# The projection up by seven block products instead of eight, on activations normed beforehand

## The chip, the core and the metric

The kernel runs on one core of one Trainium2 chip. The core has a matrix engine (TensorE, PE in the profile), a vector engine (VectorE, DVE), an engine for functions of one operand (ScalarE, ACT), a general engine (GpSimd, POOL) and a queue that starts transfers (SyncE, SP). The working memory is SBUF with 128 partitions; matrix products land in PSUM, which has eight banks of 512 fp32 columns here. The metric is the device time of one execution in microseconds; runs are compared by their median.

## The reference

A residual block of a streaming encoder on a sequence of 512 tokens behind 16 meta tokens, with model width 1024: a mixer, then a gated feed-forward network with a causal convolution of width 3, with RMS norms before each and at the end. The change concerns the feed-forward half. Cut to it:

```python
def rms_norm(x, gain):
    xf = x.astype(jnp.float32)
    y = xf * lax.rsqrt(jnp.mean(xf * xf, axis=-1, keepdims=True) + RMS_EPS)
    return (y * gain.astype(jnp.float32)).astype(x.dtype)

def conv_ffn(h, w_up, conv_w, conv_b, w_down):
    u = causal_dwconv(h @ w_up.astype(h.dtype), conv_w, conv_b)
    gate, up = u[..., :D_FF], u[..., D_FF:]          # D_FF = 2816
    return (jax.nn.silu(gate) * up) @ w_down.astype(h.dtype)
...
        h = h + hybrid_mixer(rms_norm(h, norm_mix_w[layer]), ...)
        h = h + conv_ffn(rms_norm(h, norm_ffn_w[layer]), ffn_w_up[layer], ffn_conv_w[layer],
                         ffn_conv_b[layer], ffn_w_down[layer])
    return rms_norm(h, norm_final_w)[:, N_META:]
```

All is fp32, and the products are made exact enough by splitting both factors.

## The kernel before

Activations lie transposed: 128 channels on the partitions, the tokens as columns. The width of 1024 is `KT` = 8 row blocks, the inner width of 2816 is `FT` = 22. Only the last `TO` = 514 of the 528 columns are still needed after the mixer (512 tokens and two for the convolution); they are worked on in two halves `HO` of 258 and 256 columns, each of which fits a PSUM bank.

Each factor of a product is split into a rounded part `hi` and a remainder `lo`. ACT writes `hi`, DVE writes `lo = raw - hi`: for weights in `weights` (L120 to L133, the lines 131 and 132), for activations in `split` (L1067). `product` (L135) then runs three matmuls per row block: hi by hi (L139), hi by lo (L140), lo by hi (L141). The pools `whi` and `wlo` (L98, L99) have two buffers each, `wraw` has three; a weight tile is 128 output channels by 1024, 512 KB, loaded by SP.

The stages that the change touches follow one another:

- Branch products (L1090 to L1146): GDN's, then fox's weights against the two branches. `ofT` holds fox's output; `mg` gathers both branches and is split to `mh`, `ml`. The first three fox tiles are begun ahead (L1124 to L1130), while the last pair of heads is still being worked on.
- Projection out (L1155 to L1169): eight tiles, each in both halves. The eviction (L1160) adds the product to the residual `h2`, which was loaded before (L1107). Then the channel gain is multiplied in (L1162), the result is split to `uh`, `ul`, and squares are summed on POOL (L1169). The factor `rstd2` of the norm (`norm_scale`, L152) is finished later, beside the first products of the next stage.
- Projection up (L1191 to L1210): for each of 22 channel blocks a gate tile and an up tile. Each takes one weight tile and 2 x 24 matmuls on `uh`, `ul`, which hold the activations without the norm's factor; the eviction on DVE multiplies it in (L1197). The convolution is one ACT and two DVE steps (L1200 to L1202), then `Silu` for the gate, the product of both on DVE (L1209), and the split to `fh`, `fl` at once.
- Projection down (L1237 to L1263): eight tiles of 22 row blocks, matmuls of 512 columns, weights in three chunks `c`; the eviction adds to `h2`, the final norm follows.

The order of each engine's instructions is made by a scheduler from priorities; without one, program order counts. Tiles in a pool wait for the release of what lay in their memory before (`reuse_waits="tile"`).

Of the kernel before, what the change touches and what calls it, by code (L numbers as in the profile page):

```python
# [12 lines left out]
F32 = mybir.dt.float32  # L13
F32R = mybir.dt.float32r
# [72 lines left out]
def hybrid_block(ctx: ExitStack, tc: tile.TileContext, xT, w_in, w_bg, w_bf, w_out, w_up, w_down,  # L87
# [10 lines left out]
    whi = ctx.enter_context(tc.tile_pool(name="whi", bufs=2))  # L98
    wlo = ctx.enter_context(tc.tile_pool(name="wlo", bufs=2))  # L99
# [35 lines left out]
    def product(ps, wh, wl, xh, xl, k0, k, a, b, first=True, last=True, w0=0):  # L135

        for i in range(k):
            ws = slice((w0 + i) * P, (w0 + i + 1) * P)
            pe.matmul(ps, wh[:, ws], xh[:, k0 + i, a:b], start=first and i == 0, stop=False)  # L139
            pe.matmul(ps, wh[:, ws], xl[:, k0 + i, a:b], start=False, stop=False)  # L140
            pe.matmul(ps, wl[:, ws], xh[:, k0 + i, a:b], start=False, stop=last and i == k - 1)  # L141
# [10 lines left out]
    def norm_scale(pl, y, parts, n):  # L152

        v = pl.tile([P, n], F32, tag="nv", bufs=1, name="nv")
        t = pl.tile([P, n], F32, tag="nt", bufs=1, name="nt")
# [6 lines left out]
        dve.scalar_tensor_tensor(y, t, 1.5, y, op0=ALU.add, op1=ALU.mult)  # L162
# [8 lines left out]
    qd = dram.tile([12, P, T], F32, name="qd")  # L171

# [779 lines left out]
    ofp = ctx.enter_context(tc.tile_pool(name="ofp", bufs=1, reuse_waits="tile"))  # L952
# [149 lines left out]
    late = ctx.enter_context(tc.tile_pool(name="late", bufs=1, reuse_waits="tile"))  # L1102
    uh = late.tile([P, KT, TO], F32R, name="uh")
    ul = late.tile([P, KT, TO], F32R, name="ul")
    h2 = late.tile([P, KT, TO], F32, name="h2")
    rstd2 = late.tile([P, TO], F32, name="rstd2")
    for k in range(KT):  # L1107
        nc.sync.dma_start(h2[:, k, :], xT[:, k, OFF:])
    with ExitStack() as bctx:
        bp = bctx.enter_context(tc.tile_pool(name="bp", bufs=1, reuse_waits="tile"))  # L1110
        rf = rb_ctx.enter_context(tc.tile_pool(name="rf", bufs=1, side="right", reuse_waits="tile"))
        ofl, ofh = (rf.tile([P, 4, TO], F32R, name=n) for n in ("ofl", "ofh"))
        mh, ml = (bp.tile([P, KT, TO], F32R, name=n) for n in ("mh", "ml"))
        for p in range(4):
            if p < 3:
                split(ofh[:, p], ofl[:, p], ofT[:, p])
            else:
                with tc.high_priority(offset=FOXP):
                    split(ofh[:, p, 0:258], ofl[:, p, 0:258], ofT[:, p, 0:258])
                    with behind(dve):  # L1120
                        last_divide(256, SEQ)
                    split(ofh[:, p, 258:], ofl[:, p, 258:], ofT[:, p, 258:])
# [25 lines left out]
        lps = ctx.enter_context(tc.tile_pool(name="lps", bufs=5, space=PSUM, reuse_waits="tile"))  # L1148
# [3 lines left out]

        acc = bp.tile([P, TO], F32, name="acc2")
        ln_exp_table()
        for e in range(KT):  # L1155
            wh, wl = weights(w_out[e].rearrange("p k c -> p (k c)"), KT, f"o{e}")
            for a, b in HO:
                ps = lbank("ps_o")
                product(ps[:, :b - a], wh, wl, mh, ml, 0, KT, a, b)
                dve.scalar_tensor_tensor(h2[:, e, a:b], ps[:, :b - a], 0.5, h2[:, e, a:b], op0=ALU.mult, op1=ALU.add)  # L1160
            ug = btmp("ug")
            act.activation(ug, h2[:, e], AF.Copy, scale=prm[:, PG_FFN + e:PG_FFN + e + 1])  # L1162
            split(uh[:, e], ul[:, e], ug)
            if e == 0:
                act.activation(acc, h2[:, e], AF.Square)
            else:
                sq = btmp("sq2")
                act.activation(sq, h2[:, e], AF.Square)
                pool.tensor_tensor(acc, acc, sq, op=ALU.add)  # L1169
        parts = []  # L1170
        for a, b in HO:
            ps = mmp.tile([P, 512], F32, tag="mm", name="ps_n2")[:, :b - a]
            pe.matmul(ps, ones, acc[:, a:b], start=True, stop=True)
            parts.append((ps, a, b))
        with tc.high_priority():
            norm_scale(bp, rstd2, parts, TO)
        note("h2", h2.rearrange("p a b -> p (a b)"))
    rb_ctx.close()
    mix_ctx.close()


    with ExitStack() as uctx:
        ap = uctx.enter_context(tc.tile_pool(name="ap", bufs=1, reuse_waits="tile"))
        u2 = uctx.enter_context(tc.tile_pool(name="u2", bufs=9, reuse_waits="tile"))
        fh = ap.tile([P, FT, SEQ], F32R, name="fh")
        fl = ap.tile([P, FT, SEQ], F32R, name="fl")

        def utmp(name):
            return u2.tile([P, TO], F32, tag="tmp", name=name)

        def up_tile(i):  # L1191
            wh, wl = weights(w_up[i].rearrange("p k c -> p (k c)"), KT, f"up{i}")
            y = utmp(f"u{i}")
            for a, b in HO:
                ps = lbank("ps_up")
                product(ps[:, :b - a], wh, wl, uh, ul, 0, KT, a, b)
                dve.tensor_tensor(y[:, a:b], ps[:, :b - a], rstd2[:, a:b], op=ALU.mult)  # L1197
            w = prm[:, PG_FC + 3 * i:PG_FC + 3 * i + 3]
            o = utmp(f"v{i}")[:, 0:SEQ]
            act.activation(o, y[:, 2:], AF.Identity, scale=w[:, 2:3], bias=prm[:, PG_FB + i:PG_FB + i + 1])  # L1200
            dve.scalar_tensor_tensor(o, y[:, 1:TO - 1], w[:, 1:2], o, op0=ALU.mult, op1=ALU.add)
            dve.scalar_tensor_tensor(o, y[:, 0:SEQ], w[:, 0:1], o, op0=ALU.mult, op1=ALU.add)  # L1202
            return o

        for f in range(FT):
            g = up_tile(2 * f)
            act.activation(g, g, AF.Silu)
            u = up_tile(2 * f + 1)
            dve.tensor_tensor(g, g, u, op=ALU.mult)  # L1209
            split(fh[:, f], fl[:, f], g)  # L1210
            if f == 0:
                note("act0", g)
# [9 lines left out]
        def residual(e, ps, a, b):  # L1222

            h3 = h2[:, e, 2 + a:2 + b]
# [3 lines left out]
            else:  # L1228
                sq = utmp("sq3")[:, 0:b - a]
# [7 lines left out]
        for e in range(KT - 1):  # L1237
# [126 lines left out]
```

## Time and profile before

| | us |
|---|---|
| median of 3 runs | 876.53 |
| lowest and highest | 873.74, 877.31 |
| the profiled execution | 877.7 |
| its span, first to last instruction | 875.8 |

The profile is of one execution. Its page gives busy times of the engines and cuts the span into forty equal slices of 21.9 us; each digit is the busy share in tenths. Other views group the instructions of a stretch by line and shape with the mean duration and the idle time ahead of them, list them in order of time, or add them up by stretch. A row of the timeline reads: start, duration, engine, line, operation, what is written from what, shapes, count, and in brackets how long the engine had been idle and what released it. Matmuls are pipelined, so that their recorded durations overlap; the distance of their starts is their cost. Of 7088 matmuls 2112 belong to the projection up.

### The profile page before, as it was taken

How to read it: one execution, taken by the hardware profiler on the slowest of the kernel's cores; microseconds unless marked ns; L12 is line 12 of the kernel's file. 1: busy time of each engine (PE TensorE's matmuls, PEld its weight loads, DVE VectorE, ACT ScalarE, POOL GpSimd, SP SyncE). 2: the span in 40 equal slices, each digit the busy share in tenths (PEclk: the TensorE clock that was granted, in tenths of full speed). 3: DMA queues.
4: the chain of work that ended last, by engine and by line, in shares of the span. 5: the costliest groups of instructions: out<-in, count | busy, mean ns of one | idle time of the engine just before them, and what ended most of it. 6: DMA issues, size and time to landing. Idle time of an engine off the chain costs nothing. (4 is left out here: it accounts for less than half of the span.)

```text
span 875.8 us, 17084 instructions
## 1 busy us (share of the span) xinstructions
PE 839.6 (96%) x7088; PEld 801.0 (91%) x7088; DVE 585.5 (67%) x1066; ACT 392.6 (45%) x611; POOL 140.5 (16%) x167
## 2 busy tenths in 40 slices
PE   7978999999999999899999999999999999999995
PEld 7977999999999999788999999999999999888884
DVE  7999998697266678787654676677766677232324
ACT  6655554523433485855354454434444344332321
POOL 4353575100000201100522100000000000010113
PEclk9999999999999999989999999999999999999997
DMA  7312233627432341335623223333223332333322
GB/s 229 107 49 73 74 97 99 149 93 176 127 116 74 92 140 61 98 103 150 218 98 97 89 83 95 97 97 95 80 92 98 97 96 77 99 91 107 91 67 96
DMA packets 52240, 91.27 MB, mean 104 GB/s; under 512 B 24438, under 2 KB 27646, under 8 KB 52164
## 3 DMA queue, kind: packets, MB, share of 16 engines
q1 hardware_dynamic: 51060, 89.14, 33.9%
q8 instruction: 55, 0.90, 0.5%
q10 hardware_dynamic: 1104, 1.05, 0.4%
q14 instruction: 21, 0.17, 0.1%
HBM read 80.01 MB, written 10.16 MB: 103 GB/s over the span
## 5 line engine op out<-in xcount | busy, mean ns | idle before, releaser
L140 PE MATMUL ps_in<-xl,hi_in 128*128 128x264 f32 (+2 forms) x720 | 197.8, 285 | 2.5 <-DVE xl L264 2.5
L139 PE MATMUL ps_in<-xh,hi_in 128*128 128x264 f32 (+2 forms) x720 | 197.4, 287 | 1.7 <-ACT hi_in L131 1.2
L140 PE MATMUL ps_up<-ul,hi_up 128*128 128x256 f32 (+1 forms) x704 | 198.7, 282 | 0.0
L141 PE MATMUL ps_in<-xh,lo_in 128*128 128x264 f32 (+2 forms) x720 | 196.7, 286 | 1.9 <-DVE lo_in L132 1.9
L141 PE MATMUL ps_up<-uh,lo_up 128*128 128x256 f32 (+1 forms) x704 | 198.4, 282 | 0.0
L139 PE MATMUL ps_up<-uh,hi_up 128*128 128x256 f32 (+1 forms) x704 | 198.0, 282 | 0.0
L140 PEld LDWEIGHTS ps_in<-xl,hi_in 128*128 128x128 f32 x720 | 132.8, 188 | 4.0 <-DVE xl L264 3.1
L139 PEld LDWEIGHTS ps_in<-xh,hi_in 128*128 128x128 f32 x720 | 132.0, 188 | 4.5 <-ACT hi_in L131 1.9
L141 PEld LDWEIGHTS ps_in<-xh,lo_in 128*128 128x128 f32 x720 | 132.0, 188 | 3.8 <-DVE lo_in L132 2.6
L139 PEld LDWEIGHTS ps_up<-uh,hi_up 128*128 128x128 f32 x704 | 133.0, 189 | 0.0
L141 PEld LDWEIGHTS ps_up<-uh,lo_up 128*128 128x128 f32 x704 | 132.8, 189 | 0.0
L140 PEld LDWEIGHTS ps_up<-ul,hi_up 128*128 128x128 f32 x704 | 132.7, 188 | 0.0
L1197 DVE TENSOR_TENSOR u<-ps_up,rstd 128x258 f32<-128x258 f32 x88 | 37.2, 425 | 56.6 <-PE ps_up L141 56.6
L139 PE MATMUL ps_dn<-fh,hi_dn 128*128 128x512 f32 (+1 forms) x198 | 73.5, 371 | 0.0
L140 PE MATMUL ps_dn<-fl,hi_dn 128*128 128x512 f32 (+1 forms) x198 | 73.0, 369 | 0.0
L141 PE MATMUL ps_dn<-fh,lo_dn 128*128 128x512 f32 (+1 forms) x198 | 73.0, 369 | 0.0
L132 DVE TENSOR_TENSOR lo_dn<-raw_dn,hi_dn 128x1024 fp32r<-128x1024 f32 (+1 forms) x25 | 29.0, 1160 | 61.2 <-ACT hi_dn L131 61.2
L131 ACT ACTIVATE hi_in<-raw_in 128x1024 fp32r<-128x1024 f32 x43 | 45.0, 1054 | 51.3 <-PE ps_in L140 33.4
L1232 POOL TENSOR_TENSOR acc<-acc,sq 128x512 f32<-128x512 f32 (+1 forms) x7 | 11.2, 1607 | 353.1 <-ACT sq L1230 353.1
L131 ACT ACTIVATE hi_up<-raw_up 128x1024 fp32r<-128x1024 f32 x44 | 46.7, 1061 | 37.8 <-PE ps_up L140 28.3
L132 DVE TENSOR_TENSOR lo_up<-raw_up,hi_up 128x1024 fp32r<-128x1024 f32 x44 | 53.9, 1225 | 14.3 <-ACT hi_up L131 14.3
L131 ACT ACTIVATE hi_dn<-raw_dn 128x1024 fp32r<-128x1024 f32 (+1 forms) x25 | 24.8, 993 | 74.9 <-PE ps_dn L140 70.0
(339 smaller groups left out, 1655.8 us busy)
## 6 DMA issues: line engine op xcount, KB each, us to landing
raw_up<-w_up SPq DMA_DIRECT2D x44, 512.0 KB, 3.5
raw_in<-w_in SPq DMA_DIRECT2D x43, 512.0 KB, 4.0
raw_dn<-w_down SPq DMA_DIRECT2D x17, 512.0 KB, 3.5
gd<-g SPq DMA_DIRECT2D x16, 257.0 KB, 4.2
gt<-gd SPq DMA_DIRECT2D x16, 257.0 KB, 2.7
raw_o<-w_out SPq DMA_DIRECT2D x8, 512.0 KB, 3.5
raw_dn<-w_down SPq DMA_DIRECT2D x8, 384.0 KB, 3.1
xr<-xT SPq DMA_DIRECT2D x8, 264.0 KB, 4.4
```

Of the source, the lines that this page charges most:

```text
L131: act.activation(hi[:, a:a + step], raw[:, a:a + step], AF.Copy)
L132: (eng or dve).tensor_tensor(lo[:, a:a + step], raw[:, a:a + step], hi[:, a:a + step].bitcast(F32), op=ALU.subtract)
L139: pe.matmul(ps, wh[:, ws], xh[:, k0 + i, a:b], start=first and i == 0, stop=False)
L140: pe.matmul(ps, wh[:, ws], xl[:, k0 + i, a:b], start=False, stop=False)
L141: pe.matmul(ps, wl[:, ws], xh[:, k0 + i, a:b], start=False, stop=last and i == k - 1)
L1197: dve.tensor_tensor(y[:, a:b], ps[:, :b - a], rstd2[:, a:b], op=ALU.mult)
L1232: pool.tensor_tensor(acc[:, a:b], acc[:, a:b], sq, op=ALU.add)
```

## The change

The 22 pairs of a gate tile and an up tile are taken as a matrix of two by two blocks: gate and up are the two block rows, the first and the last four of the eight row blocks of the width are the two block columns. The activations are two by two blocks too: the same halves of the width, by two halves of the columns, of 258 each, which overlap by two columns (0 to 258, 256 to 514). Strassen's algorithm in Winograd's form computes the four output blocks by seven block products of 4 x 3 matmuls instead of eight.

- Weights: POOL makes four sums of 512 columns per pair (`load_pair`). The operands of the seven products are a11 and a12 (chunk X, the gate tile as loaded), the third sum and a22 (Y), s2 and s1 (Z) and the fourth sum (W); each chunk is split by ACT and DVE (`split_chunk`), up to two chunks ahead.
- Activations: since sums of blocks go into the products, the norm's factor and the gain are multiplied in beforehand (`unit`), blocks are combined on DVE (`combine`), and each of the seven is split (`operand`). They stay in `MH`, `ML` for the stage.
- To have them early, the projection out leaves the second halves of its last three tiles to the end, and the norm of the first half runs meanwhile. The products 1 and 2, which need the first half alone, are run for three pairs ahead (`AHEAD`).
- PSUM: products 1, 6 and 7 are accumulated in one bank, 5 and 3 in another; in between ACT and DVE read the sums that the outputs need. PE's order is written out (`seq`, `manual_schedule`).
- The gating product goes from DVE to POOL (`F_POOL`), into `f` in fp32; its split to `fh`, `fl` is made behind the stage, since the operands fill the memory.
- `h2` is loaded later, written to DRAM (`hd`) behind the projection out and read back for the projection down. There the first two tiles run chunk by chunk in turn. The last down tile no longer loads its first chunk twice. `whi` and `wlo` are made anew with three buffers behind `ofT`'s release.

```diff
+    w_ctx.close()
+    whi = ctx.enter_context(tc.tile_pool(name="whi", bufs=3, reuse_waits="tile"))
+    wlo = ctx.enter_context(tc.tile_pool(name="wlo", bufs=3, reuse_waits="tile"))
...
+        def unit(name, k0, a, gain):
+            u = tp.tile([P, 4, HB], F32, tag="t", bufs=6, name=name)
+            for k in range(4):
+                dve.scalar_tensor_tensor(u[:, k], h2[:, k0 + k, a:a + HB], gain[:, k0 + k:k0 + k + 1], rstd2[:, a:a + HB],
+                                         op0=ALU.mult, op1=ALU.mult)
+            return u
+
+        def operand(j, u, sign=1.0):
+            for k in (slice(0, 2), slice(2, 4)):
+                act.activation(MH[j][:, k], u[:, k], AF.Copy, scale=sign)
+                if sign == 1.0:
+                    dve.tensor_tensor(ML[j][:, k], u[:, k], MH[j][:, k].bitcast(F32), op=ALU.subtract)
...
         for e in range(KT):
+            w = weights(w_out[e].rearrange("p k c -> p (k c)"), KT, f"o{e}")
+            sq = out_tile(e, *w, *HO[0])
+            if e < KT - 3:
+                out_tile(e, *w, *HO[1])
             else:
+                last[e] = w
+        ffn_norm(sq, *HO[0])
+        for e, w in last.items():
+            sq = out_tile(e, *w, *HO[1])
+            nc.sync.dma_start(hd[e], h2[:, e, 2:])
...
+        with tc.high_priority(offset=SOON_W):
+            n11 = unit("n11", 0, 0, ngain)
+            operand(1, n11)
+            b21 = unit("b21", 4, 0, gain)
+            operand(2, b21)
+        ffn_norm(sq, *HO[1])
...
+    seq = [(j, i) for i in range(AHEAD) for j in (1, 2)]
+    for i in range(FT + 1):
+        for j, d in ((1, 0), (2, 0), (7, 1), (4, 1), (6, 0), (5, 0), (3, 1)):
+            if 0 <= i - d < FT and not (j < 3 and i < AHEAD):
+                seq.append((j, i - d))
...
+    def load_pair(i):
...
+        for o, x, y in ((s1, a21, a22), (s2, s1, a11), (q3, a11, a21), (Q[i], s2, a12)):
+            pool.tensor_tensor(o, x, y, op=ALU.add)
...
+    def seven(ps, j, i, start=True):
+        wh, wl = splits[chunk_of[j], i]
+        for k in range(4):
+            ws = slice((place[j] + k) * P, (place[j] + k + 1) * P)
+            for w, x in ((wh, MH), (wh, ML), (wl, MH)):
+                pe.matmul(ps, w[:, ws], x[j][:, k], start=start and k == 0 and w is wh and x is MH,
+                          stop=k == 3 and w is wl, skip_group_check=not start)
...
+            g = conv(YG.pop(i), 2 * i)
             act.activation(g, g, AF.Silu)
+            u = conv(YU.pop(i), 2 * i + 1)
+            (pool if F_POOL else dve).tensor_tensor(f[:, i], g, u, op=ALU.mult)
...
+    b12, b22 = unit("b12", 0, HB - 2, gain), unit("b22", 4, HB - 2, gain)
...
+    t1 = combine("t1", b12, n11, ALU.add)
+    t2 = combine("t2", b22, t1, ALU.subtract)
+    operand(6, t2)
+    operand(5, t1)
+    operand(7, combine("m7", b12, b22, ALU.subtract))
+    operand(4, combine("m4", b21, t2, ALU.subtract))
+    operand(3, b22, -1.0)
...
+        for k in range(FT):
+            fh.append(ap.tile([P, SEQ], F32R, name=f"fh{k}"))
+            fl.append(ap.tile([P, SEQ], F32R, name=f"fl{k}"))
+            split(fh[k], fl[k], f[:, k])
+        h3t = ap.tile([P, KT, SEQ], F32, name="h3")
+        for e in range(KT):
+            nc.sync.dma_start(h3t[:, e], hd[e])
...
+        ps2 = [mmp.tile([P, 512], F32, tag="mm", name="ps_dn") for _ in range(2)]
+        for c in range(3):
+            for e in range(2):
+                k0, kn, (wh, wl) = down_weights(e, c)
+                product(ps2[e], wh, wl, fh, fl, k0, kn, 0, SEQ, first=c == 0, last=c == 2)
```

More of the change, by code (lines that the diff above doesn't have):

```diff
@@ L65 @@
 SOON_B = 100
+SOON_U = 400
+F_POOL = 1
 F2B = 4
+HB = 258
+AHEAD = 3
 GRP = 4
@@ L138, in product @@
             ws = slice((w0 + i) * P, (w0 + i + 1) * P)
[L139 to L141 removed]
+            h, l = (x[k0 + i][:, a:b] if isinstance(x, list) else x[:, k0 + i, a:b] for x in (xh, xl))
+            pe.matmul(ps, wh[:, ws], h, start=first and i == 0, stop=False)
+            pe.matmul(ps, wh[:, ws], l, start=False, stop=False)
+            pe.matmul(ps, wl[:, ws], h, start=False, stop=last and i == k - 1)
     def behind(eng):
@@ L1153, in hybrid_block @@
+        late = late_ctx.enter_context(tc.tile_pool(name="late", bufs=1, side="right", reuse_waits="tile"))
+        h2 = late.tile([P, KT, TO], F32, name="h2")
+        rstd2 = late.tile([P, TO], F32, name="rstd2")
+        ngain = late.tile([P, KT], F32, name="ngain")
+        for k in range(KT):
+            nc.sync.dma_start(h2[:, k, :], xT[:, k, OFF:])
+        dve.tensor_scalar(ngain, prm[:, PG_FFN:PG_FFN + KT], -1.0, None, op0=ALU.mult)
         acc = bp.tile([P, TO], F32, name="acc2")
         ln_exp_table()
-        for e in range(KT):
[L1156 to L1165, printed above, removed]
-            else:
-                sq = btmp("sq2")
-                act.activation(sq, h2[:, e], AF.Square)
-                pool.tensor_tensor(acc, acc, sq, op=ALU.add)
@@ L1170, in hybrid_block @@
[L1170 to L1212, printed above, removed]
@@ new lines, in out_tile @@
+        def out_tile(e, wh, wl, a, b):
+            ps = lbank("ps_o")
+            product(ps[:, :b - a], wh, wl, mh, ml, 0, KT, a, b)
+            dve.scalar_tensor_tensor(h2[:, e, a:b], ps[:, :b - a], 0.5, h2[:, e, a:b], op0=ALU.mult, op1=ALU.add)
+            if e == 0:
+                act.activation(acc[:, a:b], h2[:, e, a:b], AF.Square)
+                return
+            sq = bp.tile([P, HB], F32, tag="sq2", bufs=3, name="sq2")[:, 0:b - a]
+            act.activation(sq, h2[:, e, a:b], AF.Square)
+            if e < KT - 1:
+                pool.tensor_tensor(acc[:, a:b], acc[:, a:b], sq, op=ALU.add)
+            return sq
@@ new lines, in ffn_norm @@
+        def ffn_norm(sq, a, b):
+            ps = mmp.tile([P, 512], F32, tag="mm", name="ps_n2")[:, :b - a]
+            pe.matmul(ps, ones, acc[:, a:b], start=True, stop=False)
+            pe.matmul(ps, ones, sq, start=False, stop=True)
+            with tc.high_priority():
+                norm_scale(bp, rstd2[:, a:b], [(ps, 0, b - a)], b - a)
+        def unit(name, k0, a, gain):
[4 more added lines that the diff above has]
+            return u
@@ new lines, in run @@
+    def run(part):
+        for j, i in part:
+            if j == (6 if i < AHEAD else 1) and i + 1 < FT:
+                load_pair(i + 1)
+            m = chunks.index((chunk_of[j], i))
+            for n in range(m, min(m + 3, len(chunks))):
+                if chunks[n] not in splits:
+                    split_chunk(*chunks[n])
+            step(j, i)
+    load_pair(0)
+    for i in range(1, AHEAD):
+        load_gate(i)
+    manual = ExitStack()
+    manual.enter_context(tc.manual_schedule(engines={pe.engine}))
```

181 lines of the change are left out of this document (151 added, 30 removed).

## The prediction

> **What bounds the kernel now.** First the page: its head and the forty slices.
>
> ```profile
> span 875.8 us, 17084 instructions
> PE 839.6 (96%) x7088; PEld 801.0 (91%) x7088; DVE 585.5 (67%) x1066; ACT 392.6 (45%) x611; POOL 140.5 (16%) x167
> ...
> PE   7978999999999999899999999999999999999995
> ...
> DVE  7999998697266678787654676677766677232324
> ...
> POOL 4353575100000201100522100000000000010113
> PEclk9999999999999999989999999999999999999997
> ```
>
> TensorE (PE) is busy in nearly every slice, at full clock, while POOL stands almost empty through slices 22 to 33. What an edit saves on PE is saved outright, as long as PE stays the slowest. Next the busy times by stretch: projection out, projection up, projection down. The columns are the length, then busy time and count of PE, of its weight loads, of DVE, ACT and POOL.
>
> ```profile
> 437.70:486.40 48.70, 48.70 (x410) 48.70 (x409) 25.11 (x38) 23.22 (x33) 12.23 (x11) 1.00 0.31 99
> 486.40:739.90 253.50, 253.50 (x2119) 253.39 (x2118) 177.93 (x266) 108.35 (x137) 1.29 (x1) 1.00 0.30 92
> 739.90:865.20 125.30, 123.42 (x600) 104.90 (x599) 39.25 (x44) 36.92 (x45) 16.50 (x13) 0.99 0.30 89
> ```
>
> The projection up lasts 253.5 us and PE never rests in it: 44 tiles of 48 matmuls, 5.76 us a tile. DVE works 177.9 us (70%), ACT 108.4, POOL 1.3. Then the groups of that stretch by line and form (columns: count, busy us, mean ns, idle before; the last row is from the stretch before out), the same for one tile's matmuls (min, median and max ns), and the timeline.
>
> ```profile
> L132 DVE TENSOR_TENSOR lo_up<-raw_up,hi_up 128x1024 fp32r<-128x1024 f32 x43 | 52.7, 1225 | 13.8 <-ACT hi_up L131 13.7
> L1201 DVE SCALAR_TENSOR_TENSOR v<-u,prm,v 128x512 f32<-128x512 f32 x43 | 32.0, 745 | 0.0
> L1209 DVE TENSOR_TENSOR v<-v,v 128x512 f32<-128x512 f32 x21 | 14.5, 692 | 1.4 <-ACT v L1207 0.7
> L1070 DVE TENSOR_TENSOR fl<-v,fh 128x512 fp32r<-128x512 f32 x21 | 14.3, 682 | 0.0
> ...
> L131 ACT ACTIVATE hi_up<-raw_up 128x1024 fp32r<-128x1024 f32 x43 | 45.6, 1061 | 34.7 <-PE ps_up L140 28.3 <-issue 3.3 <-PE ps_o L140 3.0
> L1200 ACT ACTIVATE v<-u,prm 128x512 f32<-128x512 f32 x43 | 34.2, 798 | 0.0
> L1207 ACT ACTIVATE v<-v 128x512 f32<-128x512 f32 x22 | 13.9, 632 | 47.3 <-DVE v L1202 47.3
> ...
> L1069 ACT ACTIVATE ofh<-ofT 128x258 fp32r<-128x258 f32 x1 | 0.4, 420 | 4.0 <-DVE ofT L1052 4.0
> ```
>
> ```profile
> L139 PE MATMUL ps_up<-uh,hi_up x704: 277/282/288, 486.5 to 739.6; 128*128 128x256 f32 x89, 128*128 128x258 f32 x87
> ...
> 734.23 0.28 PE L139 MATMUL ps_up<-uh,hi_up 128*128 128x258 f32 x1
> ...
> 737.12 0.28 PE L139 MATMUL ps_up<-uh,hi_up 128*128 128x256 f32 x1
> ...
> 735.45 1.22 DVE L132 TENSOR_TENSOR lo_dn<-raw_dn,hi_dn 128x1024 fp32r<-128x1024 f32 x1
> 736.60 0.74 DVE L1201 SCALAR_TENSOR_TENSOR v<-u,prm,v 128x512 f32<-128x512 f32 x1
> 737.32 0.43 DVE L1197 TENSOR_TENSOR u<-ps_up,rstd 128x258 f32<-128x258 f32 x1
> 737.66 0.74 DVE L1202 SCALAR_TENSOR_TENSOR v<-u,prm,v 128x512 f32<-128x512 f32 x1
> ```
>
> A matmul is recorded with 0.28 us because it is pipelined; what counts is the distance of starts. The 24 matmuls of 258 columns take 737.12 - 734.23 = 2.89 us, 0.1204 each. In the same way DVE's successive starts give 1.15 us for a split of 1024, 0.72 for a step of the conv, 0.34 for an eviction.
>
> **The change part by part.**
>
> *PE.* A pair of tiles (gate and up) has now 2 x 48 = 96 matmuls; seven products of four row blocks and three matmuls make 84, each of 258 columns: 84 x 0.1204 = 10.1 us instead of 11.5. For 22 pairs that is 222.5 us against 253.5: 31 us less, if PE goes on without a rest.
>
> *DVE and ACT, per pair.* Weights are split in chunks of 1024, 1024, 1024 and 512 instead of two of 1024; four evictions and four conv steps stay; the gating product goes to POOL, and the split of f leaves the stage. DVE: 3 x 1.15 + 0.62 (512, its 0.68 less the overlap of starts) + 4 x 0.72 + 4 x 0.34 = 8.3 us. ACT: 3 x 1.06 + 0.63 + 2 x 0.80 + 0.63 and three copies of 258 at 0.42: 7.3. Each alone fits into 10.1.
>
> *POOL, per pair.* Four sums of weight blocks and the gating product, each 512 columns from two SBUF inputs. Whether POOL can do them beside DVE is shown by rows of other stages:
>
> ```profile
> 450.42 0.69 DVE L1070 TENSOR_TENSOR ul<-ug,uh 128x514 fp32r<-128x514 f32 x1
> ...
> 460.24 1.29 POOL L1169 TENSOR_TENSOR acc<-acc,sq 128x514 f32<-128x514 f32 x1 [4.47 <-ACT sq L1168]
> ...
> 460.91 0.43 DVE L1160 SCALAR_TENSOR_TENSOR h<-ps_o,h 128x258 f32<-128x258 f32 x1 [0.70 <-PE ps_o L141]
> ...
> 488.90 1.29 POOL L1169 TENSOR_TENSOR acc<-acc,sq 128x514 f32<-128x514 f32 x1 [4.45 <-ACT sq L1168]
> ...
> 489.38 1.37 DVE L1070 TENSOR_TENSOR ul<-ug,uh 128x514 fp32r<-128x514 f32 x1 [0.44 <-ACT uh L1069]
> ...
> 770.99 1.23 DVE L132 TENSOR_TENSOR lo_dn<-raw_dn,hi_dn 128x1024 fp32r<-128x1024 f32 x1 [0.18 <-ACT hi_dn L131]
> ...
> 771.56 1.82 POOL L1232 TENSOR_TENSOR acc<-acc,sq 128x512 f32<-128x512 f32 x1 [281.36 <-ACT sq L1230]
> ```
>
> Alone, DVE's split of 514 takes 0.69. Begun inside a POOL sum it takes 1.37 and ends at 490.75, 0.56 after the sum's end at 490.19: it stood until POOL was done. The other way round, the POOL sum begun inside a DVE split ends at 773.38, 1.16 after the split's end at 772.22. But the eviction at 460.91, with one input in PSUM, takes its usual 0.43 in the midst of a POOL sum. So a DVE instruction with both tensors in SBUF and a POOL instruction exclude each other, and PSUM evictions don't take part. POOL holds what they share for about 1.15 us per sum. DVE holds it for (1225 - 682)/512 = 1.06 ns an element. Per pair DVE has 3584 elements of splits and 2048 of conv: 5.97 us; POOL has 5 x 1.15 = 5.75. **Together 11.7 us, more than PE's 10.1**, in whatever order they come. That is the crux: before, POOL had 1.3 us in the whole stage.
>
> DVE works in order, so a split that stands holds up evictions behind it, and PE waits for both. End to end it would be 8.3 + 5.75 = 14.06. Off go the evictions that can run under POOL, at most 4 x 0.34 = 1.36, and the start-up of five held instructions, 5 x 0.14 (1.225 less 1024 x 1.06 ns): 12.0. I take **12.0 a pair**, near the lower end, and keep 11.7 and 14.06.
>
> The Trainium skill, "SBUF — State Buffer", section "Who interferes with whom", says that a DVE instruction with two SBUF inputs contends with a GpSimd instruction that reads SBUF, and that the later one fully blocks until the first is finished. The trace agrees in kind (1.37 against 0.69) and is milder in size; the rule taken for whole recorded times is the third rival.
>
> *The edge out to up.* Norm and operands now stand ahead of the products. The chain of waits at the kernel's end shows the way from a last matmul to a finished rstd (its first row, one matmul of 512 columns, is for the next edge):
>
> ```profile
> 857.12 0.21 PE ps_dn L141
> ...
> 865.03 0.13 PE ps_dn L141
> ...
> 866.11 0.71 PE ps_n L1257 x2
> ...
> 868.71 0.43 DVE rstd L162
> ```
>
> 869.14 - 865.03 = 4.1 us, then n11 (4 x 0.34) and its split (ACT 0.63, DVE 2 x 0.62): 7.4. The first half's chain lies under three half tiles of out, 3 x 2.89 = 8.7 us, so the first product waits little. After out's end DVE owes: eviction and norm 5 x 0.43, b12 and b22 8 x 0.34, four combinations and five splits of 2 x 0.62 each: 16.1 us, of which the six first products (8.7 us of PE) hide a part if PE sets the pace, and none if DVE does. Two X splits fall before out's end (2.3) and the last pair's conv behind the last product (2.9): 5.2 off.
>
> *h2, hd, weights.* Rows for what moves on the DMA queue:
>
> ```profile
> 445.18 0.69 DVE L1070 TENSOR_TENSOR ml<-mg,mh 128x514 fp32r<-128x514 f32 x1 [1.20 <-ACT mh L1069]
> ...
> 447.54 0.76 DVE L1160 SCALAR_TENSOR_TENSOR h<-ps_o,h 128x258 f32<-128x258 f32 x2 [1.67 <-PE ps_o L141]
> ...
> raw_up<-w_up SPq DMA_DIRECT2D x44, 512.0 KB, 3.5
> ...
> xr<-xT SPq DMA_DIRECT2D x8, 264.0 KB, 4.4
> ```
>
> h2 may now load only when mg is read out, at 445.87; at 4.4 us it lands by 450.3, after the first eviction's time 447.54. Five banks of 2.89 us cover the 2.8 us: nothing; without them 2.8. Weights queued behind those eight loads on SP have three raw tiles in hand. The spill and reload of h2 (2 x 2.1 MB) go into queues with a 0.30 share: nothing. The same weights are read.
>
> *The new split buffers.* The pools of hi and lo are laid out anew with three buffers, the second and third lo in the memory of ofT, whose last reader is this split:
>
> ```profile
> 421.82 0.42 DVE L1070 TENSOR_TENSOR ofl<-ofT,ofh 128x256 fp32r<-128x256 f32 x1 [0.48 <-ACT ofh L1069]
> ```
>
> The third fox tile, begun ahead as filler (18 matmuls of 0.12, 2.2 us), needs its lo weights in there, so they come after 422.24. If nothing else fills PE then, 2.2 us are lost; at the least nothing. I take 2.
>
> *The edge up to down.* fh and fl take the operands' memory, the third pair of them that of product 3, the last. PE has two row blocks of down ready, 6 x 0.21, then waits for ACT 0.63 and DVE 0.68 behind the last evictions; afterwards DVE's 0.62 a block keeps step with PE's 0.64. Bounds 0, and 8.7 if the reload of h2 stands on SP ahead of the first down weights (conv 2.9, landing 3.5, split 1.06 and 1.23). I take 3. One down load fewer at the end is off the path.
>
> *Sum.* Stage 22 x 12.0 + 16.1 - 5.2 = 274.9, 21.4 more than 253.5; with 3 at the lower edge and 2 at the buffers, 26.4 more. The profiled execution took 877.7 us, 1.9 outside its span and 1.2 above the median of 876.53: 904.1, as a median **903**. By port time alone: 22 x 11.7 + 12.0 (the operands' 11352 elements) - 5.5 = 263.9, so 892 with both edges and 887 without. By 14.06 it is 320.2, so 948.
>
> **The rivals.**
>
> *PE sets the pace: faster.* If POOL's hold were shorter in this stage, or fell into DVE's gaps, PE would run at 10.1: 222.5, a wait of some 8 for the operands (16.1 less 8.7 of cover), 5 at the edges, 18 less: 858. It decides where the pair's shared time falls under 10.1, POOL's hold under (10.1 - 5.97)/5 = 0.83; break-even is (253.5 - 5 - 10.9)/22 = 10.8 a pair, a hold of 0.97. For it speaks that few POOL rows stand in a stage like this; against it, both rows above.
>
> *Gain and wait cancel: no change.* A pair of 10.6 to 11.0 us: 877. It needs a hold of about 1 us and a smooth order.
>
> *Whole blocking: slower still.* DVE finds nothing to do while POOL works, and recorded times add: 5 x 1.29 + 3 x 1.225 + 0.68 + 4 x 0.745 = 13.8 a pair, 314.5 in the stage, 942. The page "SBUF — State Buffer" of the Trainium skill gives this case.
>
> *It does less than it says.* If a product of 258 columns cost more than 0.1204 us, as the first of an accumulation into a used bank, the 31 us would shrink; the up row shows 277 to 288 ns for every form, so I count this within the others.
>
> **How the numbers follow.** Forecast (885 to 925) 0.56; PE's pace 0.28; no change 0.08; whole blocking 0.08. The range 858 to 928 leaves out half of the PE case and most of the last: 0.2. This kernel's measurement can tell 0.5% from no change, 872 to 881. Faster 0.28, same 0.08, slower 0.64.
>
> **What would show it.** Right: PE busy near 80% in the up stage, its idle time ended by DVE's lo splits and evictions; POOL sums of 1.6 to 2.3 us instead of 1.29, conv steps and splits with means well over 0.745 and 1.225; evictions still 0.43. Wrong: a pair in 10.1 us, or POOL at 1.29 throughout beside a busy DVE. A first wait of 8 us and then none would leave only the edges' price. A gap of 8 us ahead of the first down matmul would mean the SP order.

## The result

| | us |
|---|---|
| before, median of 4 runs beside the change | 876.92 (873.74 to 877.88) |
| after, median of 4 runs | 955.77 (953.23 to 958.71) |
| ratio | 1.0907, 95% interval 1.0865 to 1.0949 |
| the profiled execution after, its span | 953.23, 951.4 |

The kernel became 9% slower, where 903 was forecast with a range of 858 to 928. The sign was right, the size was not: 75.5 us more between the two profiled executions instead of 26.4.

First the head of the page after the change, with the slices that answer to those shown of before:

```profile
span 951.4 us, 17010 instructions
PE 846.1 (89%) x6828; PEld 798.4 (84%) x6828; DVE 690.2 (73%) x1121; ACT 443.8 (47%) x727; POOL 349.6 (37%) x282
...
PE   8979999999999998989984978878988887799994
...
DVE  7999799783655778857369889888887798922223
...
POOL 4441673000000211106326777766776681101012
PEclk9999999999999999999997899989888999899998
```

PE has holes in the projection up, and POOL, idle there before, is busy in 65% of it (209.8 of 322.6 us). The windows by stage (length, then busy time and count of PE, its weight loads, DVE, ACT, POOL; granted clock) show where the time went:

```profile
436.80:492.40 55.60, 55.60 (x463) 55.45 (x461) 26.85 (x45) 20.34 (x32) 21.05 (x22) 1.00 0.49 163
492.40:815.00 322.60, 256.29 (x1855) 248.13 (x1853) 275.68 (x309) 156.17 (x241) 209.81 (x111) 0.89 0.25 81
815.00:940.20 125.20, 123.08 (x597) 103.92 (x598) 45.49 (x57) 43.82 (x61) 13.88 (x14) 0.99 0.31 93
```

The projection up takes 322.6 us instead of 253.5, 69.1 more. Out ends at 492.4 instead of 486.4, another 6.0, and what follows the stage is 0.5 longer (951.4 - 815.0 against 875.8 - 739.9). Down is as before. What a steady pair takes is read from one instruction that occurs once in it, the split of the gate tile (min, median and max ns, first and last start):

```profile
L1294 DVE TENSOR_TENSOR lo_X<-raw_g,hi_X x12: 1218/1220/1221, 582.0 to 733.6; 128x1024 fp32r<-128x1024 f32 x12
```

Twelve splits, eleven pairs: (733.6 - 582.0) / 11 = **13.78 us a pair**, where 12.0 was forecast and 11.52 was the time before. The steady stretch from 560 to 740 us as a window, its groups (count, busy us, mean ns, idle before) and its waits (us, times, longest):

```profile
560.00:740.00 180.00, 153.20 (x1124) 149.55 (x1123) 152.25 (x161) 85.02 (x132) 127.23 (x66) 0.91 0.23 77
```

```profile
L1294 DVE TENSOR_TENSOR lo_Z<-S,hi_Z 128x1024 fp32r<-128x1024 f32 x14 | 27.6, 1972 | 0.1
...
L1316 DVE SCALAR_TENSOR_TENSOR v<-yg,prm,v 128x512 f32<-128x512 f32 x14 | 25.0, 1782 | 0.0
...
L1316 DVE SCALAR_TENSOR_TENSOR v<-yu,prm,v 128x512 f32<-128x512 f32 x13 | 9.8, 751 | 27.7 <-ACT v L1315 27.7
...
L1358 DVE TENSOR_TENSOR yg<-n,ps_c 128x258 f32<-128x258 f32 x14 | 5.8, 412 | 0.0
```

```profile
ACT v L1315 <- POOL f L1362: 68.5, 13, 6.6
POOL S L1285 <- DMA raw_u<-w_up: 49.1, 12, 4.6
PEld ps_c L1304 <- DVE yu L1349: 27.9, 13, 3.3
DVE v L1316 <- ACT v L1315: 27.7, 12, 3.3
PE ps_c L1304 <- DVE yu L1349: 25.2, 12, 3.1
```

The exclusion is plain: the split of chunk Z takes 1972 ns instead of 1225, the gate's first conv step 1782 instead of 745 (the up tile's, which comes while POOL is idle, 751), and an eviction, with one input in PSUM, 412 as ever. Time in which an instruction stands, held by the other engine, counts as busy in these records. So DVE is busy, stands included, in 152.25 of the 180 us, 11.7 us of a pair, which is no more than the 12.0 of the forecast. But there are also waits that the forecast had not: DVE is idle 2.1 us a pair until ACT has done a conv step, ACT waits 5.3 at a time for POOL's gating product, and POOL 4.1 at a time for a load. Which of the three makes the pair long, the profile alone doesn't say. One pair in order of time (start, duration, engine, what, idle before):

```profile
604.25 1.73 POOL L1362 TENSOR_TENSOR f<-v,v 128x512 f32<-128x512 f32 x1
...
606.01 0.81 ACT L1315 ACTIVATE v<-yu,prm 128x512 f32<-128x512 f32 x1 [5.38 <-POOL f L1362]
606.73 0.61 ACT L1293 ACTIVATE hi_W<-Q 128x512 fp32r<-128x512 f32 x1
606.86 0.75 DVE L1316 SCALAR_TENSOR_TENSOR v<-yu,prm,v 128x512 f32<-128x512 f32 x1 [2.02 <-ACT v L1315]
...
607.53 0.68 DVE L1294 TENSOR_TENSOR lo_W<-Q,hi_W 128x512 fp32r<-128x512 f32 x1
...
608.13 0.42 DVE L1349 TENSOR_TENSOR yu<-u,ps_c 128x258 f32<-128x258 f32 x1
```

The product of one pair ends at 605.98, and only then may ACT write the conv output of the next pair's up tile; the split of chunk W and the eviction of `ps_c`, on which PE waits, stand behind it.

### The profile page after: what moved, and what is told of

Same layout as the page of the kernel before. It is cut to its first block, busy times and chain, and to the rows that moved or that the text cites. A ratio compares the mean times of both kernels' runs of the same rounds, so it can differ in the third digit from the quotient of the medians.

```text
span 951.4 us, 17010 instructions
## 1 busy us (share of the span) xinstructions
PE 846.1 (89%) x6828; PEld 798.4 (84%) x6828; DVE 690.2 (73%) x1121; ACT 443.8 (47%) x727; POOL 349.6 (37%) x282
## 3 DMA queue, kind: packets, MB, share of 16 engines
q10 hardware_dynamic: 1104, 1.05, 0.3%
## 4 chain that ended last, share of the span: by engine, by line
PE 65%; DVE 17%; ACT 7%; issue 3%; POOL 3%; DMA 3%; SPq 0%; DVEq 0%; ACTq 0%; POOLq 0%
PE ps_a L1304 8%; PE ps_in L147 6%; PE ps_in L145 6%; PE ps_in L146 6%; PE ps_c L1304 5%; PE ps_dn L146 4%; PE ps_dn L147 4%; PE ps_dn L145 4%; PE ps L846 2%; PE ps_b L1304 2%; PE ps_d L1304 2%; DMA raw_u<-w_up 2%; PE ps_o L146 2%; PE ps_o L145 2%; PE ps_o L147 2%
## 5 line engine op out<-in xcount | busy, mean ns | idle before, releaser
L1285 POOL TENSOR_TENSOR S<-raw_u 128x512 f32<-128x512 f32 x22 | 48.4, 2201 | 88.7 <-DMA raw_u<-w_up 76.4
L474 POOL PARTITION_ALL_REDUCE mb<-mx x8 | 15.4, 1927 | 173.2 <-ACT osq L881 84.4
L1304 PE MATMUL ps_c<-mh,hi_W 128*128 128x258 f32 x88 | 30.2, 343 | 37.6 <-DVE yu L1349 37.5
L1315 ACT ACTIVATE v<-yu,prm 128x512 f32<-128x512 f32 x22 | 17.9, 814 | 95.6 <-POOL f L1362 95.6
L1304 PEld LDWEIGHTS ps_c<-mh,hi_W 128*128 128x128 f32 x88 | 19.5, 221 | 41.5 <-DVE yu L1349 39.8
L137 DVE TENSOR_TENSOR lo_in<-raw_in,hi_in 128x1024 fp32r<-128x1024 f32 x39 | 49.1, 1260 | 4.3 <-ACT hi_in L136 4.2
L145 PEld LDWEIGHTS ps_dn<-fh,hi_dn 128*128 128x128 f32 x198 | 37.7, 191 | 12.3 <-ACT fh L1077 6.3
L1437 POOL TENSOR_TENSOR acc<-acc,sq 128x512 f32<-128x512 f32 (+1 forms) x7 | 8.5, 1210 | 107.3 <-ACT sq L1435 107.3
L1285 POOL TENSOR_TENSOR raw_u<-raw_g,raw_u 128x512 f32<-128x512 f32 x22 | 46.8, 2129 | 0.0
L1316 DVE SCALAR_TENSOR_TENSOR v<-yu,prm,v 128x512 f32<-128x512 f32 x22 | 16.5, 750 | 39.5 <-ACT v L1315 39.5
```

The lines of the kernel that those rows point to most:

```text
L137: (eng or dve).tensor_tensor(lo[:, a:a + step], raw[:, a:a + step], hi[:, a:a + step].bitcast(F32), op=ALU.subtract)
L145: pe.matmul(ps, wh[:, ws], h, start=first and i == 0, stop=False)
L474: pool.partition_all_reduce(mb, mx, P, ReduceOp.max)
L1285: pool.tensor_tensor(o, x, y, op=ALU.add)
L1304: pe.matmul(ps, w[:, ws], x[j][:, k], start=start and k == 0 and w is wh and x is MH, stop=k == 3 and w is wl, skip_group_check=not start)
L1315: act.activation(o3, y[:, :, 2:], AF.Identity, scale=w[:, 2:3], bias=prm[:, PG_FB + i:PG_FB + i + 1])
```

## The experiments

Each was a change to one of the two kernels. Unless more are named, a run has one time; the kernel before, run beside it on the same chip, took 876.1 to 878.7 us. That kernel's times in all runs spread from 873.7 to 878.7, so differences of 1 to 3 us between single runs say little.

**Is it the load of the up weights?** The timeline invited this reading: `raw_u` stands on SP behind a gate load that waits for POOL's Q sum (raw_g issued 604.31, raw_u 604.74), and POOL's next sums wait for `raw_u`.

```diff
-        nc.sync.dma_start(U[i].rearrange("p (a b) -> p a b", b=H4)[:, 0:3:2], WU[2 * i + 1].rearrange("p (a b) -> p a b", b=H4))
+        nc.scalar.dma_start(U[i].rearrange("p (a b) -> p a b", b=H4)[:, 0:3:2], WU[2 * i + 1].rearrange("p (a b) -> p a b", b=H4))
```

> The load of the up weights (raw_u) is issued from ACT's queue instead of SP's, where it stood behind the load of a later gate tile that waits for POOL's Q sum. Theory 'load loop' (in the changed kernel raw_u lands 5.0 us after a Q sum ends and POOL's four sums and the product then take 8.7 us, which makes the 13.7 us of a pair): the loop is cut, POOL no longer waits for raw_u, the steady pair falls to the shared time of 11.7 to 12.5 us, and with some 18 steady pairs the time to 920 to 935 us. Rival 'port and order alone' (DVE and POOL exclude each other and the order of their instructions makes 13.6 us, the load only arrives late because POOL was late): POOL's waits for raw_u go, but the pair stays at 13.3 to 13.7 and the time at 945 to 957 us.

Measured 948.7 us; the same split runs from 586.0 to 733.2 in eleven pairs, 13.38 us each. The rival's 945 to 957 came, but POOL's waits for `raw_u` did not go, as both readings had said. Two of the waits of this run, 560 to 740 us:

```profile
ACT n L1328 <- PE ps_b L1304: 28.0, 9, 3.7
POOL S L1285 <- DMA raw_u<-w_up: 27.7, 8, 7.5
```

The load now holds up ACT, in whose queue it stands: it is issued at 604.75, right behind the DVE split of a Y chunk that frees its buffer (ends 604.71), and ACT goes on at 605.34, after 3.72 us idle. So one wait was exchanged for another. This run makes the load loop unlikely and doesn't settle it; the run with the buffers alone, below, does.

**Is it the exclusion?** Sums, then sums and product, moved to DVE; then only two of the sums; then no sums at all.

```diff
-            pool.tensor_tensor(o, x, y, op=ALU.add)
+            dve.tensor_tensor(o, x, y, op=ALU.add)
```

> The four weight sums of each pair run on DVE; POOL keeps the gating product alone. Theory 'exclusion' (a sum on POOL takes the shared port for 1.15 us and DVE stands meanwhile): a sum on DVE costs 0.62 us of DVE's own time and no one's else, DVE has 8.3 + 4 x 0.62 = 10.8 us a pair, and with the product's hold 10.8 to 12.0; the conv and split rows go back towards 0.75 and 1.23 us, the time falls by 22 x (13.6 less 10.8 to 12.0) to 895 to 920 us. Rival 'load loop': here the sums wait for raw_u as before, only on DVE; it would keep a pair near 5.0 + 4 x 0.62 plus the wait for DVE's other work, so it gives the same or less and PE waits show lo_Z and lo_W; above 935 us it would be neither.

Measured 909.87 us, (737.8 - 575.2) / 14 = 11.61 a pair. The groups of the same stretch in this kernel:

```profile
L1285 DVE TENSOR_TENSOR Q<-S,raw_g 128x512 f32<-128x512 f32 x16 | 27.7, 1734 | 0.0
...
L1294 DVE TENSOR_TENSOR lo_Z<-S,hi_Z 128x1024 fp32r<-128x1024 f32 x15 | 18.2, 1211 | 0.0
...
L1285 DVE TENSOR_TENSOR S<-S,raw_g 128x512 f32<-128x512 f32 x16 | 10.9, 678 | 0.0
```

Three of the four sums take 680 ns, splits their old 1211; only the Q sum, which meets POOL's product (1296 ns), takes 1734, 1.05 more. One POOL instruction makes one DVE instruction stand.

With `F_POOL = 0` besides:

> The sums and the gating product all run on DVE, POOL is empty in the stage. Theory 'exclusion': no DVE row is stretched any more (conv 0.745, splits 1.225), DVE is full with 8.3 + 5 x 0.62 = 11.4 us a pair, so the pair takes 11.4 to 11.9 and the time is 22 x 1.7 to 2.2 us less, 905 to 920. Rival 'the product on POOL holds ACT and so PE': this kernel then is faster than the one with the product left on POOL by 10 us or more; by exclusion alone the two lie within 10 us of each other.

Measured 905.23 us, 4.6 less than with the product left on POOL. So the product alone doesn't hold ACT and PE: that rival had 10 us or more. This kernel is the fastest of the versions that compute the reference; four more times of it:

> The same kernel as in the run with sums and product on DVE (905.2 us in one look), now timed in rounds, as the fastest of the versions that compute the reference: 903 to 909 us, a ratio of 1.029 to 1.037 to the kernel before; DVE with 11.2 us a pair and the edges' 30 us stay.

Measured 906.19, a ratio of 1.0324 (1.0307 to 1.0341) to before. DVE's own rate, from the same split as above:

```profile
L1294 DVE TENSOR_TENSOR lo_X<-raw_g,hi_X x16: 1209/1218/1221, 575.2 to 743.3; 128x1024 fp32r<-128x1024 f32 x16
```

(743.3 - 575.2) / 15 = 11.21 us a pair, with DVE busy in 176.3 of the 180 us from 560 to 740. Without the five instructions at 0.62 that leaves 8.1, near the 8.3 of the forecast.

> Of the four sums the two into S run on DVE; q3, Q and the gating product stay on POOL, three POOL instructions a pair. Theory 'end to end': a 512-column instruction moved from DVE to POOL costs a pair 1.05 - 0.62 = 0.43 us, 9.5 us in 22 pairs; from 905.2 (none on POOL) over 909.9 (one) that gives 924 to 934 here, about midway to the changed kernel. Rival 'shared time alone' (evictions run beside POOL and only the instructions with both inputs in SBUF count): 5.97 + 2 x 0.53 + 3 x 1.15 = 10.5 us a pair, so DVE's own 8.1 + 2 x 0.62 and PE set the pace and the time is 900 to 912.

```diff
+            (dve if x is a21 or x is s1 else pool).tensor_tensor(o, x, y, op=ALU.add)
```

Measured 926.03 us, (738.6 - 581.3) / 13 = 12.10 a pair. "End to end" had 924 to 934 us, but its price, 8.1 + 2 x 0.62 + 3 x 1.05 = 12.5 a pair, is more than was measured.

> The weight sums are left out: the products take the weight blocks as they are loaded (the output is not that of the reference), with the same 84 matmuls, splits, evictions and conv steps a pair and the gating product on POOL. It shows what a pair takes without the sums. By 'exclusion' the shared time is 5.97 + 1.15 = 7.1 us, PE sets the pace with 10.1 to 10.5 us a pair, and the time is 22 x 3.1 to 3.5 less: 878 to 890 us. If something other than the sums holds the pair (the evictions' order, the conv, ACT's order), the pair stays above 11.5 us and the time above 905.

```diff
-        for o, x, y in ((s1, a21, a22), (s2, s1, a11), (q3, a11, a21), (Q[i], s2, a12)):
-            pool.tensor_tensor(o, x, y, op=ALU.add)
+        nc.sync.dma_start(U[i][:, H4:], WU[2 * i + 1])
...
-        src = {"X": lambda: G[i], "Y": lambda: U[i][:, H4:], "Z": lambda: S[i], "W": lambda: Q[i]}[c]()
+        src = {"X": lambda: G[i], "Y": lambda: U[i][:, H4:], "Z": lambda: G[i], "W": lambda: U[i][:, H4:2 * H4]}[c]()
```

Measured 880.15 us against 878.68 of before. Its pairs:

```profile
L1288 DVE TENSOR_TENSOR lo_X<-raw_g,hi_X x14: 2009/2014/2270, 582.4 to 713.7; 128x1024 fp32r<-128x1024 f32 x14
```

(713.7 - 582.4) / 13 = 10.10 us: PE's pace, 84 x 0.1204. The 31 us on PE are real. That the kernel is no faster even so shows a second loss, as large, outside the steady pairs.

**Is it ACT's wait for the product?** The conv's output has three buffers, two of them per pair, and POOL's product reads them last.

```diff
-        o = yp.tile([P, SEQ], F32, tag="v", bufs=3, name=f"v{i}")
+        o = yp.tile([P, SEQ], F32, tag="v", bufs=5, name=f"v{i}")
```

First together with the load on ACT's queue, then alone:

> As the run with raw_u on ACT's queue (948.7 us), and besides five buffers instead of three for the conv's output, so that ACT's first conv step no longer waits for POOL's gating product. Theory 'end to end' (each of the five POOL instructions of a pair makes DVE stand for 1.05 us, as the one product does in the run with the sums on DVE, where the sum begun under it takes 1734 ns instead of 680; nothing of it is hidden, and DVE's own 8.1 us come on top): 8.1 + 5 x 1.05 = 13.3 us a pair whatever the order, so 938 to 949 us and DVE busy over 93% of the steady stretch. Rival 'waits in order' (ACT's and the loads' waits make the pair): with both gone the pair falls to 11.7 to 12.3 us and the time to 915 to 925.

> The changed kernel with five buffers instead of three for the conv's output and nothing else; raw_u stays on SP's queue. With raw_u on ACT's queue the time was 948.7 us, with both edits 931.4 (12.5 us a pair, DVE busy in 99% of the stretch). Theory 'two waits in a row' (either wait alone is enough to hold the pair): this edit alone brings little, 945 to 956 us, and POOL still waits for raw_u some 4 us a pair. Rival 'ACT's wait is the one that counts': the pair falls to 12.5 to 12.8 us and the time to 930 to 938.

Measured 931.38 and 932.42 us. The first lies between the two ranges that were expected of it. The steady stretch with the buffers alone, as window, pairs and waits; the waits are from 560 to 720 us, the changed kernel's first:

```profile
560.00:740.00 180.00, 156.19 (x1228) 150.85 (x1229) 180.00 (x176) 97.49 (x147) 124.07 (x70) 0.99 0.25 83
```

```profile
L1294 DVE TENSOR_TENSOR lo_X<-raw_g,hi_X x14: 1211/1214/1982, 581.8 to 744.0; 128x1024 fp32r<-128x1024 f32 x14
```

```profile
POOL S L1285 <- DMA raw_u<-w_up: 40.0, 10, 4.5
...
POOL S L1285 <- DMA raw_u<-w_up: 47.9, 12, 4.7
```

DVE is busy in all 180 us, stands included, and a pair takes (744.0 - 581.8) / 13 = 12.48. ACT's wait for the product is gone from the list; POOL waits for `raw_u` as long as before, 4.0 us at a time. So the 1.3 us a pair belong to the buffers; neither "two waits in a row" nor the load by itself explains the 13.78. What is left of the load's wait costs little: with the load on ACT's queue besides, POOL's wait for it is 25.5 us in the same stretch and the pair 12.28. Five buffers instead of three are worth 20.8 us (953.2 - 932.4). The "waits in order" rival was half right: 12.3 to 12.5 came, between its 11.7 to 12.3 and the 13.3 of "end to end", whose 1.05 us an instruction was too much.

**Does the exclusion show in the kernel before?**

```diff
             act.activation(g, g, AF.Silu)
+            for _ in range(2):
+                pool.tensor_tensor(spare, g, acc0[:, 0:SEQ], op=ALU.add)
             u = up_tile(2 * f + 1)
+            for _ in range(3):
+                pool.tensor_tensor(spare, u, acc0[:, 0:SEQ], op=ALU.add)
```

> The kernel before, and in its projection up five POOL additions of 512 columns for each pair of tiles, into a tile that nobody reads (so nothing waits for them); each reads a finished conv output, which paces them. DVE has there 177.9/22 = 8.1 us of its own a pair, of which 5120 elements with both inputs in SBUF (5.43 us), and PE takes 11.52. Theory 'end to end': 8.1 + 5 x 1.05 = 13.3 us a pair, DVE becomes the slowest, and the kernel before takes 22 x 1.8 = 40 us more, 905 to 925 us. Rival 'shared time alone': 5.43 + 5 x 1.15 = 11.2 us, still under 11.52, and the time stays at 877 to 885. Rival 'no exclusion': 877 and DVE rows unstretched.

Measured 915.11 us, 38.9 more, for sums that nobody waits for. Its groups in the projection up:

```profile
L132 DVE TENSOR_TENSOR lo_up<-raw_up,hi_up 128x1024 fp32r<-128x1024 f32 x43 | 80.2, 1865 | 26.6 <-ACT hi_up L131 26.6
L1203 DVE SCALAR_TENSOR_TENSOR v<-u,prm,v 128x512 f32<-128x512 f32 x42 | 71.7, 1710 | 1.4 <-ACT v L1202 1.4
```

Splits of 1225 and the first conv steps of 745 are stretched by the same 0.6 to 1.0 us as in the changed kernel. So the exclusion shows here too. The number of "end to end" came (the stage takes 290.1 us, 13.2 a pair), but not by its mechanism: DVE is not full, it is busy in 248.2 of the 290.1 us and waits 26.6 for ACT's `hi`. Its busy time grew by 70.3 us for 110 additions, 0.64 each.

> The kernel before with five POOL copies of 512 columns for each pair (one input in SBUF) in place of the five additions (two inputs) that made it 915.1 us. If what POOL and DVE exclude each other by is taken by any POOL instruction on SBUF for its whole length, the time is again 22 x 5 x (0.87/1.29 of a copy's length) of DVE's time more, 890 to 915 us; if only POOL instructions with two inputs take it, the time stays at 876 to 882 and DVE's rows are unstretched.

Measured 875.25 us, no change. This run decides nothing: the expectation left out DVE's slack. DVE has 8.1 of 11.52 us to do, and five copies of 615 ns at two thirds would add 2.1, still under PE's pace. The copies do hold DVE a little (the split of f takes 913 ns instead of 682 in the stage).

**The edges.** Without sums PE sets the pace, so that what is lost at the edges is read from its waits. The timeline of PE at the entry of the projection up in the run without sums:

```profile
496.71 0.55 PE L1298 MATMUL ps_a<-mh,hi_X 128*128 128x258 f32 x1 [2.80 <-DVE h L1183]
...
510.54 0.39 PE L1298 MATMUL ps_a<-mh,hi_Z 128*128 128x258 f32 x1 [1.55 <-ACT mh L1210]
516.15 0.58 PE L1298 MATMUL ps_a<-ml,hi_Z 128*128 128x258 f32 x1 [5.22 <-DVE ml L1212]
```

Out ended at 493.1 there; eight products (96 matmuls, 11.6 us) were done at 520.6. So the entry costs 27.5 - 11.6 = 15.9 us. Of these 8.8 lie at the two Z products, which took 11.7 us from the end of the sixth product instead of 2.9. The other 7.1 are the wait for the norm and what follows it: 3.6 us until the first product, and behind the gap matmuls 0.21 apart instead of 0.12 until 502.6, at a granted clock of 0.50 from 496.7 to 502.

```diff
-                pe.matmul(ps, w[:, ws], x[j][:, k], start=start and k == 0 and w is wh and x is MH,
+                pe.matmul(ps, w[:, ws], x[1 + j % 2][:, k], start=start and k == 0 and w is wh and x is MH,
...
-    b12, b22 = unit("b12", 0, HB - 2, gain), unit("b22", 4, HB - 2, gain)
...
-    operand(6, t2)
-    operand(5, t1)
...
```

> As the run without sums (880.15 us), and the operands of products 3 to 7 are left out too: b12, b22, the four combinations and the five splits behind the six first products; these products read operand 1 or 2 instead (the output is not that of the reference). It shows what DVE's debt at the entry of the projection up costs when PE sets the pace after it. In the run without sums the first Z product began 1.7 us late and it and the next took 10.0 us instead of 2.9: theory 'the debt': both go, 8.8 us less, 869 to 873 us. Rival 'norm and clock' (the wait for rstd2 and the slow clock after it make the entry): 876 to 880.

Measured 870.92 us, 9.2 less, where 8.8 was expected; beside the kernel before on its own chip it is 6.8 less. The traces show what of it is the debt. Out ends at 491.4 here, and the eight products are done when the next one begins:

```profile
511.76 0.29 PE L1298 MATMUL ps_a<-mh,hi_Y 128*128 128x258 f32 x1
```

That is 20.4 us behind out's end instead of 27.5: the debt of operands is worth 7.1 us. The waits at the Z products are gone, as the theory said, but the wait for the norm and the slow clock behind it take 8.8 here instead of 7.1. Of the 9.2, 1.7 lie ahead of the entry, where this edit changes nothing; that the sum came out so near 8.8 is luck.

At the lower edge the very first split of f stands on ACT behind the last pair's Silu (run without sums):

```profile
737.98 0.63 ACT L1354 ACTIVATE v<-v 128x512 f32<-128x512 f32 x1 [2.25 <-DVE v L1311]
738.52 0.61 ACT L1077 ACTIVATE fh<-f 128x512 fp32r<-128x512 f32 x1
```

```diff
+            if i == FT - 1:
+                for k, e in enumerate(early):
+                    split(*e, f[:, k])
```

> The run without sums (880.15 us, output not that of the reference), and the first six blocks of the gating product are split into hi and lo as soon as they are written, into memory of their own, instead of behind the last pair's Silu in ACT's order. Theory 'ACT's order' (at the lower edge PE stands some 6 to 8 us because the very first split of f is queued on ACT behind the last pair's conv and Silu): the first product of the projection down begins at once behind the last of the projection up, with 18 matmuls of 0.21 us in hand, 3.8 us, and the time falls by 3 to 4 us, to 876 to 877. Rival 'weights or banks' (the down weights or a PSUM bank are what comes last there): the gap ahead of the first down matmul stays and the time with it, 879 to 882.

Measured 874.88 us (median of 8), a ratio of 0.9987 (0.9966 to 1.0008) to before. That is 5.3 under the run without it, and 2.7 if each is taken against the kernel before on its own chip; in the traces, the last gate split is 147.3 us ahead of the last down matmul instead of 152.9, 5.6 less. The first down matmul:

```profile
L145 PE MATMUL ps_dn<-fhe,hi_dn x12: 390/394/404, 730.3 to 739.5; 128*128 128x512 f32 x12
```

It begins at 730.3, ahead even of the last up product, instead of 739.2. Neither the weights nor a bank held it, so ACT's order made that gap.

The upper edge was not tried. Its windows, after and then before, show PE's idle time of 3.7 us beside the last pair of heads:

```profile
416.00:420.00 4.00, 2.24 (x24) 1.73 (x24) 1.04 (x4) 1.64 (x4) 0.00 (x0) 1.00 0.01 4
420.00:424.00 4.00, 2.02 (x9) 1.85 (x10) 3.52 (x6) 0.42 (x1) 0.00 (x0) 0.81 0.15 18
```

```profile
416.00:420.00 4.00, 4.00 (x43) 3.69 (x42) 0.54 (x2) 0.15 (x1) 0.00 (x0) 1.00 0.19 75
420.00:424.00 4.00, 4.00 (x35) 4.00 (x35) 2.37 (x7) 0.84 (x2) 0.91 (x2) 1.00 0.76 231
```

What filled this time before were the fox tiles begun ahead. Their lo weights come late now, those of all three, behind the last split of `ofT`, which begins at 420.83 (after; then the first two before):

```profile
421.17 3.49 DVE L137 TENSOR_TENSOR lo_bf<-raw_bf,hi_bf 128x1024 fp32r<-128x1024 f32 x3
...
404.09 1.22 DVE L132 TENSOR_TENSOR lo_bf<-raw_bf,hi_bf 128x1024 fp32r<-128x1024 f32 x1 [0.56 <-ACT hi_bf L131]
...
412.83 1.21 DVE L132 TENSOR_TENSOR lo_bf<-raw_bf,hi_bf 128x1024 fp32r<-128x1024 f32 x1
```

## Why the prediction was wrong

The 75.5 us between the profiled executions, split up by the runs (mostly differences of single times, so good to 1 to 3 us):

| term | forecast | measured | from |
|---|---|---|---|
| PE, 22 pairs | -31 | -31.3 | 10.10 a pair without sums |
| sums, product and DVE, 22 pairs | +41.5 (264 - 222.5) | +52.3 | 932.42 - 880.15 |
| ACT's wait for the product | 0 | +20.8 | 953.23 - 932.42 |
| entry, lower edge, buffers and behind | +15.9 | +33.7 | what is left |
| sum | +26.4 | +75.5 | |

The last row but one is a remainder. It agrees with what the run without sums shows by itself: entry 15.9, lower edge 7.9 (1.7 us in front of the last product and 6.2 behind it), out 6.6, from the first down matmul on 3.3.

*PE: right.* 84 matmuls at 0.1204 us, no loss within a pair once the operands are there.

*The failed step: "I take 12.0 a pair", "in whatever order they come".* It took the pair to be DVE's time alone. In the changed kernel that time is 11.7 us, near the forecast, and the pair is 13.78, because DVE also waits 2.1 us; a wait of this kind stands at nothing in the sum. The gating product was moved to POOL with a price for the port and none for a wait, though it became the last reader of the conv's buffers. Three of them, two per pair, mean that ACT can't write the second one of a pair before POOL, behind four sums of a later pair, has read those of the pair before. ACT works in order, so the W split, DVE's split behind it and the eviction for PE stood too. Five buffers take this wait away, and a steady pair falls by 1.3 us. Before, the product ran on DVE next to the conv with nine buffers.

A second term was too small. With the wait gone DVE is full, and the pair is 12.48, not 12.0: the forecast's 12.0 is 8.3 and five times 0.74, this run's 12.48 is 8.1 and five times 0.87. The 0.87 comes from the pairs with no POOL instruction (11.21) and with five (12.48): each one moved away from DVE, where it costs 0.62, adds 1.27 / 5 = 0.25; the pairs with one (11.61) and with three (12.10) lie 0.15 and 0.13 above that line. It is no fixed price: 0.71 comes from the 11.7 us of the changed kernel, and 0.64 from the additions in the kernel before, where DVE was idle part of the time.

*The rival "whole blocking" hit the pair's number and not the cause.* It said 13.8 a pair from recorded durations, and 13.78 came; that is luck. With five buffers the pair falls to 12.48 with the same five POOL instructions: whole blocking is not what happens. The Trainium skill, "SBUF — State Buffer", section "Who interferes with whom", calls what DVE and GpSimd share an exclusive lock, and has the order of issue decide who blocks. The run with one POOL instruction a pair agrees (1734 ns against 680). The price in the pair, 0.87 of 1.29 us, is smaller; that evictions run beside POOL (412 ns as ever) and starts of held instructions too would make it so, by the forecast's own sum, but no run separates the two.

*The entry: 10.9 us of debt where DVE sets the pace, "a wait of some 8" where PE does.* Where PE does, 15.9 was measured. The debt itself (7.1 to 8.8) was well put; left out was that the norm's wait, costed at "little", comes on top and leaves PE at a clock of 0.50 for some 5 us.

*The lower edge: 3, measured 7.9.* The bounds had been 0 and 8.7, with SP's order as the way to the upper one. A gap of 8 us ahead of the first down matmul was to mean "the SP order"; one of 6.2 came, and the cause was ACT's order. The forecast had two row blocks of down ready, which supposed that early blocks of f are split early.

*Buffers and h2: 2, measured some 6 in the end of out.* The forecast had the third fox tile alone come late; the lo weights of all three did. So more than its 2.2 us of filler was lost, and the clock of 0.81 behind the idle time was not foreseen either. This is only read from the trace; whether memory or DVE's order holds the first two is open.

*What was to show each step* came: PE at 79% of the stage (256.3 of 322.6), sums of 1.8 to 2.3 us, the gate's conv steps and the splits of Y and Z far above their means, evictions at 0.41. None of these tells the exclusion from the buffer wait; DVE's idle 2.1 us a pair does, and the forecast had not asked for it.

## What to carry to other kernels

An instruction moved to another engine carries its buffers with it: count how many instructions stand on the new engine between the write and the last read, and give the writer buffers for that long (five instead of three took the wait away here). Two-input work moved from a full DVE to POOL was no relief here (0.87 us of DVE's time against 0.62). And the gain of a shorter loop (31 us) has to be set against its edges, each in-order queue's tail among them: here they took 33.7.

## What the runs showed of the hardware

- PE's granted clock fell in the steady stretch without any single long gap: 0.91 over 560 to 740 us in the changed kernel, whose waits there were at most 3.1 us, and 0.99 with five buffers.
- An addition of 512 columns takes POOL 1.29 us when nothing holds it (the shortest of those added to the kernel before), a copy 0.62 (the median of those put in their place).
- A wait of an engine can last as long after a cure as before: from 560 to 720 us POOL was idle 40.0 us in 10 waits for `raw_u` in the slow kernel, and 47.9 in 12 waits in the one 20.8 us faster.
